# A two-layer diffusion step on one core: constants on other queues, finer first pieces of the modulation, its loads a batch ahead of their products

## The chip, the cores and the metric

One Trainium2 chip, one of its cores. The time is device microseconds (us) of one execution of the whole program, and the figure for a kernel is the median of its runs.

## The reference

Two layers over 256 tokens of 2048 columns: 128 context tokens (group 0) and 128 latent tokens (group 1). All weights are fp32 and each is used once in a step. Cut to what matters here:

```
mod    = silu(c) @ w_mod + b_mod                 # w_mod: 2048 x 12288 a layer; six segments of 2048
shift1, scale1, gate1, shift2, scale2, gate2 = split(mod, 6)
h      = rmsnorm(x, norm1) * (1 + scale1) + shift1
proj   = h @ w_in                                # 2048 x 4640
mix    = concat(attention(proj), gated_linear_attention(proj)) @ w_out      # 2048 x 2048
x      = x + gate1 * mix
h2     = rmsnorm(x, norm2) * (1 + scale2) + shift2
x      = x + gate2 * (relu(h2 @ w_up) ** 2 @ w_down)      # 2048 x 8192 and back
```

The two groups have conditioning vectors of their own (`c_ctx` and `c`). Nothing of a layer's projection can start before shift1 and scale1 of the columns that it contracts over are there.

## The kernel before

**Weights.** A weight matrix is read in chunks of 256 rows and 512 columns (512 KB) into `raw`, one of eight buffers of the pool `rawp`. `split` (L106 to 108) makes two fp32r parts of a chunk: ScalarE rounds it (`wh`, L107), VectorE subtracts (`wl`, L108). `block` (L304) computes 512 output columns: for each chunk and each group, six products into a PSUM tile `acc`, namely `wh` with the high and the low part of x (`TH`, `TL`; L345, L346) and `wl` with `TH` (L347), for two rows of 128. A full block of eight chunks has 96 such products.

**Modulation.** `w_mod` goes through the same eight buffers as `rawm`, on the same SyncE queue. A load of 512 KB feeds two products of 32 columns of TensorE (L219, L237). The generator `on_pe` yields after each load and its products; `pump` advances it by so many loads. `block` calls it beside its chunks, in batches of at least `BATCH` = 4, by a share per block that the table `N_MOD` sets for each stage; `need` advances it until what is asked for is there. `mod_first` (L227) makes shift1 and scale1 of layer 0 in four quarters of four 128-row chunks; `mod_pe` (L209) makes a segment of 2048 columns in 32 loads. Layer 0's segments 2, 4 and 3 and layer 1's 4 and 3 are made in this way; the others are summed by VectorE beside the MLP (`mod_dve`, L254).

**Stages of layer 0.** The head: constants, silu of the conditioning vectors, x normalised and transposed into `xT0` (L397 to 411), the first quarter of the modulation. Stage a: nine blocks of `w_in` over chunk rows 0 to 3, then nine over rows 4 to 7, kept as partial sums `part` (L427, L429). Stage b: the nine blocks over rows 8 to 15, with attention and linear attention as side work of the blocks. Then the output projection (four blocks of `w_out`, the second norm behind the last of them), and the MLP. In layer 1 the projection is one stage, c, of nine full blocks.

**What sets the order.** SyncE issues every weight load, in program order as the scheduler of the build left it. Each engine executes its own list in order. A load waits for the buffer that it takes over, and the loads of the SyncE and ScalarE queues share eight completion semaphores in turn, so that the ninth load waits until the first has landed. GpSimd's queue carries masks, x, head norms and caches (`load`, L68). The lists of the engines are shown below where the change moves them.

Of the kernel before, what the change touches and what calls it, by code (L numbers as in the profile page):

```python
# [50 lines left out]
def trunk(tc, nc, I, O):  # L51
    with ExitStack() as st:
# [18 lines left out]
        # tiles of 4 KB a partition; a tag's slots are shared by tiles that live one after the other  # L71
# [19 lines left out]
        nc.sync.dma_start(ident, I["ident"])  # L91
# [5 lines left out]
        # column 1 of ones: from column 1 - g on it sums over the partitions into row g  # L97
# [12 lines left out]
        def rstd(ss, n, count):  # L110
            """(ss / count + EPS) ** -0.5: by exp and log, then a Newton step"""
# [20 lines left out]
        crow = etile((32, P), "crow")  # L132
        nc.sync.dma_start(crow[0:16], I["c_ctx"].rearrange("(k p) -> k p", p=P))
        nc.sync.dma_start(crow[16:32], I["c"].rearrange("o (k p) -> (o k) p", p=P))
# [9 lines left out]
        # columns (k, g); a product takes 32 of them from (k, 0) on and uses its first two rows  # L144
# [4 lines left out]
        # per layer: columns of b_mod, norm1, norm2 and of the gate biases  # L149
        cols, gcols, modc, gdram = [], [], [], []  # L150
        for l in range(L):
            rows = etile((P, P), "rows")
            nc.sync.dma_start(rows[0:96], I["b_mod"][l].rearrange("(k p) -> k p", p=P))
            nc.sync.dma_start(rows[96:112], I["norm1"][l].rearrange("(k p) -> k p", p=P))
            nc.sync.dma_start(rows[112:128], I["norm2"][l].rearrange("(k p) -> k p", p=P))
            grow = etile((8, P), "grow")
            nc.sync.dma_start(grow[0:4], I["b_gate_fwd"][l].rearrange("(k p) -> k p", p=P))
            nc.sync.dma_start(grow[4:8], I["b_gate_bwd"][l].rearrange("(k p) -> k p", p=P))
# [9 lines left out]
        # modulation: a segment of 2048 columns, as columns of modc; either all on the tensor engine, or  # L168
        # with the sums over the row chunks on the vector engine
# [20 lines left out]
        def mod_turn(ps):  # L190
            """four transposes in place"""
            pt = ps.rearrange("p (j t) -> p j t", t=P)
            for h in range(2):
# [4 lines left out]
            return pt  # L198
# [11 lines left out]
        def mod_pe(l, seg):  # L210
            ps = ps_mod.tile([P, 512], F32, tag="mod", name="mod")
            for kc in range(KC):
                for half in range(2):
# [3 lines left out]
                    for cc in range(2):  # L217
                        q = half * 2 + cc
                        nc.tensor.matmul(ps[32 * q:32 * q + 32, :], CT[:, 2 * kc:2 * kc + 32], raw[:, cc * 512:(cc + 1) * 512],  # L219
                                         start=kc == 0, stop=kc == KC - 1)  # L220
                    if kc < KC - 1 or half < 1:
                        yield
            mod_columns(l, seg, ps)
            yield

        def mod_first(l, q):
            """a quarter of the columns of shift1 and scale1, in sums over the even and over the odd row chunks"""  # L227
            ps = ps_mod.tile([P, 512], F32, tag="mod", name="mod")
            for ch in range(KC // 2):
                for a in range(2):  # L230
                    raw = rawp.tile([P, 2, 512], F32, tag="raw", name="rawm")
                    c0 = a * D + q * 512
                    nc.sync.dma_start(raw, I["w_mod"][l, ch * 256:(ch + 1) * 256, c0:c0 + 512]
                                      .rearrange("(c p) n -> p c n", p=P))
                    for k in range(2):
                        r = 32 * (a * 2 + k)
                        nc.tensor.matmul(ps[r:r + 32, :], CT[:, 4 * ch + 2 * k:4 * ch + 2 * k + 32], raw[:, k],  # L237
                                         start=ch == 0, stop=ch == KC // 2 - 1)
                    if ch < KC // 2 - 1 or a < 1:
                        yield  # L240
            pt = mod_turn(ps)
            pv = pt.rearrange("p j (c r) -> p c r j", r=32)
            ks = slice(q * 4, q * 4 + 4)
            for a in range(2):
                m = modc[l][:, a, :, ks]
# [46 lines left out]
        def pump(gen, n=1):  # L292
            for _ in range(n):
                next(gen, None)
# [602 lines left out]
```

## Time and profile before

| | |
|---|---|
| runs | 2413.26, 2414.18, 2421.23 us; median 2414.18 |
| profiled execution, first to last instruction | 2416.7 us (the trace gives no time for it beside this span) |
| TensorE busy | 2352.2 us, 97% of the span |
| granted TensorE clock, mean | 0.990 |
| moved by DMA | 613.20 MB, mean 254 GB/s |

How to read it: a busy TensorE row is not TensorE at its peak, since the records of matmuls overlap; the distance from the start of one to the start of the next says what one costs. The profiled execution lies 2.5 us above the median of the runs.

### The profile page before, as it was taken

To read this page: it belongs to the slowest core of one execution; us is meant where nothing else is said; L and a number is where in the kernel's file an instruction comes from. 1 tells how busy PE (TensorE), PEld (TensorE's weight loads), DVE (VectorE), ACT (ScalarE), POOL (GpSimd) and SP (SyncE) were. 2 spreads that over 40 slices of the span, in tenths; PEclk is the share of its full clock that TensorE was granted. 3 is DMA by queue.
4 is the path that set the end of the run, shared out by engine and by line. 5 is a ranking of instruction groups with operands and counts; after the bars stand their busy time and mean duration, and the time that the engine had idled before them with its cause. 6 is when DMAs were issued, how large, how long until landed. Compare 5 with 4: busy or idle time off the path is not lost.

```text
span 2416.7 us, 32872 instructions
## 1 busy us (share of the span) xinstructions
PE 2352.2 (97%) x12533; PEld 1778.1 (74%) x12533; DVE 1635.4 (68%) x1936; ACT 1090.3 (45%) x1470; POOL 192.0 (8%) x253
## 2 busy tenths in 40 slices
PE   6999999989999999999999999999999999999998
PEld 2655555767878878878876767777788888888887
DVE  3444774558998999959976675556898445454455
ACT  2423443545544534534544555455554443443542
POOL 1000341100000000000010432010000000000001
PEclk9999999998999999999999999999999999999999
DMA  8899878885889989858887577788688656656654
GB/s 299 270 335 332 288 277 281 284 290 191 297 301 310 303 278 309 296 184 296 302 273 256 184 233 230 245 263 263 227 287 279 190 177 202 189 183 191 193 179 182
DMA packets 274334, 613.20 MB, mean 254 GB/s; under 512 B 24273, under 2 KB 24785, under 8 KB 274177
## 3 DMA queue, kind: packets, MB, share of 16 engines
q1 hardware_dynamic: 264048, 579.63, 72.2%
q0 software_dynamic: 10128, 31.48, 4.4%
q8 instruction: 98, 1.61, 0.3%
q14 instruction: 60, 0.48, 0.1%
HBM read 601.01 MB, written 10.03 MB: 253 GB/s over the span
## 4 chain that ended last, share of the span: by engine, by line
PE 86%; DVE 4%; DMA 4%; issue 3%; POOL 1%; ACT 1%; SPq 0%; POOLq 0%; DVEq 0%; ACTq 0%
PE acc L345 25%; PE acc L347 25%; PE acc L346 25%; PE mod L219 4%; PE mod L237 2%; DVE wl L108 1%; DMA rawm<-in_w_mod_dram 1%; DMA raw<-in_w_up_dram 1%; PE aT L104 1%; DMA raw<-in_w_down_dram 1%; DVE ga L270 1%; DMA rows<-in_b_mod_dram 1%; PE sc L577 1%; PE mod L277 1%; PE xnT L104 1%
## 5 line engine op out<-in xcount | busy, mean ns | idle before, releaser
L108 DVE TENSOR_TENSOR wl<-raw,wh 128x1024 fp32r<-128x1024 f32 (+1 forms) x586 | 692.1, 1189 | 423.6 <-ACT wh L107 407.4
L107 ACT CAST wh<-raw 128x1024 fp32r<-128x1024 f32 (+1 forms) x586 | 592.4, 1017 | 785.1 <-PE acc L346 623.8
L345 PE MATMUL acc<-wh,TH 128*128 128x512 f32 x2248 | 892.8, 398 | 1.1 <-ACT wh L107 1.0
L346 PE MATMUL acc<-wh,TL 128*128 128x512 f32 x2248 | 882.5, 393 | 0.4 <-DVE TL L108 0.4
L347 PE MATMUL acc<-wl,TH 128*128 128x512 f32 x2248 | 862.4, 396 | 1.6 <-DVE wl L108 1.6
L345 PEld LDWEIGHTS acc<-wh,TH 128*128 128x128 f32 x2248 | 423.7, 189 | 139.5 <-issue 27.3
L347 PEld LDWEIGHTS acc<-wl,TH 128*128 128x128 f32 x2248 | 422.8, 189 | 126.4 <-issue 16.6
L346 PEld LDWEIGHTS acc<-wh,TL 128*128 128x128 f32 x2248 | 423.9, 189 | 94.0 <-issue 6.8
L270 DVE SCALAR_TENSOR_TENSOR ga<-rawm,CT,ga 128x1024 f32<-128x1024 f32 x300 | 378.1, 1278 | 28.8 <-DMA rawm<-in_w_mod_dram 27.7
L108 DVE TENSOR_TENSOR wx<-raw,wx 128x1024 fp32r<-128x1024 f32 (+1 forms) x182 | 194.5, 1079 | 102.8 <-ACT wx L107 102.7
L107 ACT CAST wx<-raw 128x1024 fp32r<-128x1024 f32 (+1 forms) x182 | 168.0, 937 | 192.6 <-PE acc L346 146.2
L345 PE MATMUL acc<-wx,TH 128*128 128x512 f32 x632 | 247.6, 392 | 0.0
L346 PE MATMUL acc<-wx,TL 128*128 128x512 f32 x632 | 246.9, 391 | 0.0
L347 PE MATMUL acc<-wx,TH 128*128 128x512 f32 x632 | 239.6, 390 | 0.0
L345 PEld LDWEIGHTS acc<-wx,TH 128*128 128x128 f32 x632 | 119.5, 189 | 25.9 <-issue 0.8
L346 PEld LDWEIGHTS acc<-wx,TL 128*128 128x128 f32 x632 | 119.4, 189 | 25.1
L347 PEld LDWEIGHTS acc<-wx,TH 128*128 128x128 f32 x632 | 119.2, 189 | 25.1
L219 PE MATMUL mod<-rawm,CT 128*32 128x512 f32 x640 | 115.8, 610 | 4.4 <-DMA rawm<-in_w_mod_dram 2.5
L237 PE MATMUL mod<-rawm,CT 128*32 128x512 f32 x256 | 58.2, 653 | 18.9 <-DMA rawm<-in_w_mod_dram 18.9
L185 POOL DMA_DIRECT2D gd<-gs x4 | 2.1, 522 | 884.6 <-DVE gs L184 884.6
L219 PEld LDWEIGHTS mod<-rawm,CT 128*32 128x32 f32 x640 | 18.9, 109 | 45.0 <-issue 40.0
L812 ACT ACTIVATE relu<-acc 128x512 f32<-128x512 f32 x64 | 37.9, 592 | 30.4 <-PE acc L347 30.4
(242 smaller groups left out, 1343.2 us busy)
## 6 DMA issues: line engine op xcount, KB each, us to landing
rawm<-in_w_mod_dram SPq DMA_DIRECT2D x384, 512.0 KB, 5.5
raw<-in_w_up_dram SPq DMA_DIRECT2D x256, 512.0 KB, 4.6
raw<-in_w_down_dram SPq DMA_DIRECT2D x256, 512.0 KB, 5.3
raw<-in_w_in_dram SPq DMA_DIRECT2D x144, 512.0 KB, 5.3
raw<-in_w_out_dram SPq DMA_DIRECT2D x64, 512.0 KB, 7.8
gx<-gd POOLq DMA_DIRECT2D x32, 256.0 KB, 7.3
x1d<-x POOLq DMA_DIRECT2D x16, 256.0 KB, 5.0
gx<-x1d POOLq DMA_DIRECT2D x16, 256.0 KB, 8.6
```

What stands on the lines that cost most here:

```text
L104: nc.tensor.transpose(dst[:, j], s, ident)
L107: nc.scalar.copy(hi, v)
L108: nc.vector.tensor_tensor(out=lo, in0=v, in1=hi.bitcast(F32), op=ALU.subtract)
L219: nc.tensor.matmul(ps[32 * q:32 * q + 32, :], CT[:, 2 * kc:2 * kc + 32], raw[:, cc * 512:(cc + 1) * 512], start=kc == 0, stop=kc == KC - 1)
L237: nc.tensor.matmul(ps[r:r + 32, :], CT[:, 4 * ch + 2 * k:4 * ch + 2 * k + 32], raw[:, k], start=ch == 0, stop=ch == KC // 2 - 1)
L270: nc.vector.scalar_tensor_tensor(out=ga[g], in0=raw, scalar=c, in1=ga[g], op0=ALU.mult, op1=ALU.add)
L277: nc.tensor.matmul(ps[32 * q:32 * q + 32, :], unit[:, 1 - g:33 - g], acc[q // 2][g][:, (q % 2) * 512:(q % 2) * 512 + 512], start=g == 0, s ...
L345: nc.tensor.matmul(acc[g], xh, wh[:, k, :], start=first, stop=False)
L346: nc.tensor.matmul(acc[g], xl, wh[:, k, :], start=False, stop=False)
L347: nc.tensor.matmul(acc[g], xh, wl[:, k, :], start=False, stop=final)
L577: nc.tensor.matmul(sps[hh][w_ * c:w_ * c + w_, n], EB[r, n % 4, j0:j0 + w_], EA[r, n % 4, i0:i0 + w_], start=True, stop=True, tile_positio ...
L812: nc.scalar.activation(r, acc, AF.Relu)
```

## The change

Three things. The identity and the conditioning vectors are loaded from ScalarE's queue and the rows of biases and norms from GpSimd's (into one tile, `rowt`); x is loaded from SyncE's queue, ahead of the first `w_mod` load. `mod_first` makes pieces of 2, 2, 4, 4 and 4 row chunks (a load of a piece of two is 512 rows of 256 columns, still 512 KB), and stage a has three rounds of nine blocks, over 1, 1 and 2 chunks. The generators yield the products as a function: `pump` first runs those of the loads issued before (`flush`), then issues new loads. The shares in `N_MOD` are new.

```diff
-N_MOD = dict(a=(2, 4), b=9.25, out0=4, c=6, out1=3)
+N_MOD = dict(a=(1, 2, 3.6), b=7, out0=8.25, c=6, out1=3)
+FIRST = ((0, 2), (2, 4), (4, 8))
 BATCH = 4
...
-        nc.sync.dma_start(ident, I["ident"])
+        nc.scalar.dma_start(ident, I["ident"])
...
-        nc.sync.dma_start(crow[0:16], I["c_ctx"].rearrange("(k p) -> k p", p=P))
-        nc.sync.dma_start(crow[16:32], I["c"].rearrange("o (k p) -> (o k) p", p=P))
+        rowt = big("PM", (P, 8, P), "rowt")
+        crow = rowt[0:32, 0]
+        nc.scalar.dma_start(crow[0:16], I["c_ctx"].rearrange("(k p) -> k p", p=P))
+        nc.scalar.dma_start(crow[16:32], I["c"].rearrange("o (k p) -> (o k) p", p=P))
+        x0 = []
+        for g, n in enumerate(("x_prompt", "x_sample")):
+            x0.append([big("E", name="x0") for _ in range(2)])
+            for h in range(2):
+                nc.sync.dma_start(x0[g][h], I[n][0][:, h * 1024:(h + 1) * 1024])
...
-            nc.sync.dma_start(rows[0:96], I["b_mod"][l].rearrange("(k p) -> k p", p=P))
+            load(rows[0:96], I["b_mod"][l].rearrange("(k p) -> k p", p=P))
...
-        on_pe = mods([(mod_first, 0, q) for q in range(4)]
+        on_pe = mods([(mod_first, 0, k0, k1 - k0) for k0, k1 in FIRST + ((8, 12), (12, 16))]
...
+        loaded = []
+
+        def flush():
+            while loaded:
+                loaded.pop(0)()
 
         def pump(gen, n=1):
+            if gen is on_pe:
+                flush()
             for _ in range(n):
-                next(gen, None)
+                products = next(gen, None)
+                if products is not None:
+                    loaded.append(products)
 
         def need(*what):
             gen = on_dve[0] if what in ON_DVE[0] else on_dve[1] if what in ON_DVE[1] else on_pe
+            if gen is on_pe and what not in have:
+                flush()
             while what not in have:
-                pump(gen)
+                pump(gen, BATCH if gen is on_pe else 1)
+                if gen is on_pe:
+                    flush()
...
-        for q in range(4):
-            need(0, "first", q)
...
+        for i, (k0, k1) in enumerate(FIRST):
+            first(k0, k1)
             for c0 in PIECES:
...
-                block(TH, TL, I["w_in"][0][:, c0:c0 + 512], None, keep, N_MOD["a"][q], [2 * q, 2 * q + 1])
+                block(TH, TL, I["w_in"][0][:, c0:c0 + 512], None, keep, N_MOD["a"][i], list(range(k0 // 2, k1 // 2)))
+        for k0 in (8, 12):
+            first(k0, k0 + 4)
```

SyncE's list at the start. Before, from the second layer's rows of constants on (the same five for layer 0 stand ahead of them, three `w_mod` loads ahead of those, and the identity and the conditioning vectors first of all):

```order
L153 DMA rows<-in_b_mod_dram 96x128
L154 DMA rows<-in_norm_dram 16x128
L155 DMA rows<-in_norm_dram 16x128
L157 DMA grow<-in_b_gate_fwd_dram 4x128
L158 DMA grow<-in_b_gate_bwd_dram 4x128
L233 DMA rawm<-in_w_mod_dram 128x2x512 x13
L320 DMA raw<-in_w_in_dram 128x2x512 x4
L233 DMA rawm<-in_w_mod_dram 128x2x512 x4
```

The same queue in the changed kernel, from its first load on:

```order
L142 DMA x_106<-in_x_prompt_dram 128x1024
L142 DMA x_107<-in_x_prompt_dram 128x1024
L142 DMA x_110<-in_x_sample_dram 128x1024
L142 DMA x_111<-in_x_sample_dram 128x1024
L244 DMA rawm<-in_w_mod_dram 128x4x256 x8
L351 DMA raw<-in_w_in_dram 128x2x512 x4
L244 DMA rawm<-in_w_mod_dram 128x4x256 x4
L351 DMA raw<-in_w_in_dram 128x2x512 x4
```

No constant stands on this queue any more, and the first chunk of `w_in` is its thirteenth load.

ScalarE's list at the start, in which `junk` are the sums of squares of x (x_151, x_152 are the prompt's halves, x_208, x_209 the sample's), `y` the two steps of the root, `wh` the rounding of a chunk of `w_in`, `xv` and `TH` the modulated x. Before:

```order
L387 ACTIVATE junk,ss<-x_151 128x512 x2
L387 ACTIVATE junk,ss<-x_152 128x512 x2
L115 ACTIVATE y<-v 128x1
L116 ACTIVATE y<-y 128x1
L387 ACTIVATE junk,ss<-x_208 128x512 x2
L387 ACTIVATE junk,ss<-x_209 128x512 x2
L115 ACTIVATE y<-v 128x1
L116 ACTIVATE y<-y 128x1
L107 CAST wh<-raw 128x1024 x3
L379 ACTIVATE xv<-xT_150,modc_130 128x128 x4
```

The changed kernel (x_110, x_111 are the sample's halves):

```order
L117 ACTIVATE y<-v 128x1
L118 ACTIVATE y<-y 128x1
L109 CAST wh<-raw 128x1024
L418 ACTIVATE junk,ss<-x_110 128x512
L109 CAST wh<-raw 128x1024
L418 ACTIVATE junk,ss<-x_110 128x512
L418 ACTIVATE junk,ss<-x_111 128x512 x2
L109 CAST wh<-raw 128x1024
L117 ACTIVATE y<-v 128x1
L118 ACTIVATE y<-y 128x1
L410 ACTIVATE xv<-xT_154,modc_136 128x128 x2
```

The roundings of the first three chunks of `w_in` now stand between and behind the sample's sums of squares, ahead of its root.

TensorE's list at the end of the third block of `w_out` in layer 0 and the start of the fourth (two rows of `mod<-rawm` are one load's products). Before:

```order
L345 MATMUL acc_4044<-wx,TH 128x512
L346 MATMUL acc_4044<-wx,TL 128x512
L347 MATMUL acc_4044<-wx,TH 128x512
L345 MATMUL acc_4232<-wh,TH 128x512
L346 MATMUL acc_4232<-wh,TL 128x512
L347 MATMUL acc_4232<-wl,TH 128x512
```

The changed kernel:

```order
L376 MATMUL acc_4064<-wx,TH 128x512
L377 MATMUL acc_4064<-wx,TL 128x512
L378 MATMUL acc_4064<-wx,TH 128x512
L230 MATMUL mod<-rawm,CT 32x512 x18
L205 MATMUL mod<-ident,modt 128x128 x4
L230 MATMUL mod<-rawm,CT 32x512 x6
L376 MATMUL acc_4312<-wh,TH 128x512
L377 MATMUL acc_4312<-wh,TL 128x512
```

Twelve loads' products and the four transposes that end a segment now stand between the two blocks; on SyncE the twelve loads stand between the last four chunks of `w_out` of the third block and the first four of the fourth.

## Rows read from the trace of the kernel before

**Rows 1.** The page: busy us, share of the span and instructions of each engine.

```profile
PE 2352.2 (97%) x12533; PEld 1778.1 (74%) x12533; DVE 1635.4 (68%) x1936; ACT 1090.3 (45%) x1470; POOL 192.0 (8%) x253
```

**Rows 2.** Windows by stage: the head, the two rounds of stage a, stage b, the output projection with the second norm. Columns: stretch, its length, busy time of PE, PEld, DVE, ACT, POOL (with counts), granted clock, DMA share, GB/s.

```profile
0.00:50.40 50.40, 26.28 (x109) 7.36 (x109) 19.65 (x53) 13.47 (x31) 8.03 (x18) 0.94 0.90 307
50.40:120.00 69.60, 69.60 (x306) 42.97 (x304) 24.61 (x31) 30.01 (x41) 0.00 (x0) 0.97 0.81 268
120.00:198.00 78.00, 76.95 (x349) 43.08 (x346) 39.39 (x61) 23.49 (x31) 0.58 (x1) 1.00 0.96 339
198.00:422.00 224.00, 217.59 (x1924) 123.76 (x1923) 135.92 (x219) 88.56 (x148) 56.54 (x62) 0.98 0.83 290
422.00:540.00 118.00, 111.58 (x534) 81.02 (x533) 69.26 (x107) 57.70 (x96) 15.96 (x29) 1.00 0.87 288
```

**Rows 3.** The timeline of TensorE in stage a at three places: start, length, line, operation.

```profile
59.91 0.39 PE L346 MATMUL acc<-wh,TL 128*128 128x512 f32 x1
60.14 0.39 PE L347 MATMUL acc<-wl,TH 128*128 128x512 f32 x1
60.45 1.07 PE L237 MATMUL mod<-rawm,CT 128*32 128x512 f32 x8
61.45 0.50 PE L345 MATMUL acc<-wh,TH 128*128 128x512 f32 x1
61.79 0.39 PE L346 MATMUL acc<-wh,TL 128*128 128x512 f32 x1
...
66.80 0.39 PE L347 MATMUL acc<-wl,TH 128*128 128x512 f32 x1
67.12 1.05 PE L237 MATMUL mod<-rawm,CT 128*32 128x512 f32 x4
68.10 0.50 PE L345 MATMUL acc<-wh,TH 128*128 128x512 f32 x1
...
157.03 0.39 PE L346 MATMUL acc<-wh,TL 128*128 128x512 f32 x1
157.35 1.92 PE L237 MATMUL mod<-rawm,CT 128*32 128x512 f32 x16
159.20 0.50 PE L347 MATMUL acc<-wl,TH 128*128 128x512 f32 x1
```

**Rows 4.** The timeline of SyncE's queue at the start: start, time until the last of the group was issued.

```profile
2.12 1.46 SPq L233 DMA_DIRECT2D rawm<-in_w_mod_dram  x3
3.62 1.24 SPq L153 DMA_DIRECT2D rows<-in_b_mod_dram  x1
18.96 0.31 SPq L155 DMA_DIRECT2D rows<-in_norm_dram  x1
19.83 0.29 SPq L158 DMA_DIRECT2D grow<-in_b_gate_bwd_dram  x1
20.16 11.51 SPq L233 DMA_DIRECT2D rawm<-in_w_mod_dram  x13
```

**Rows 5.** What SyncE's queue waited for in the first 50 us: total, times, longest.

```profile
SPq L155 <- DMA rawm<-in_w_mod_dram: 7.0, 1, 7.0
```

**Rows 6.** Windows of 4 us in the head (columns as in rows 2).

```profile
0.00:4.00 4.00, 0.00 (x0) 0.00 (x0) 0.33 (x4) 1.28 (x1) 2.93 (x9) 1.00 0.35 73
12.00:16.00 4.00, 1.58 (x4) 0.00 (x0) 0.00 (x0) 0.00 (x0) 0.90 (x2) 1.00 1.04 177
32.00:36.00 4.00, 3.85 (x24) 2.00 (x24) 3.43 (x11) 0.00 (x0) 0.00 (x0) 1.00 1.05 387
```

**Rows 7.** The timeline of the head from the sample's sums of squares to the first product of a block (all engines, lines left out).

```profile
29.86 0.61 ACT L387 ACTIVATE junk<-x 128x512 f32<-128x512 f32 x1
31.26 0.14 DVE L113 TENSOR_SCALAR v<-s 128x1 f32<-128x1 f32 x1
32.50 1.67 DVE L408 TENSOR_SCALAR xn<-x,r 128x512 f32<-128x512 f32 x4
34.09 1.28 DVE L411 COPY xT<-xnT 128x512 f32<-128x512 f32 x2
...
43.07 1.04 ACT L107 CAST wh<-raw 128x1024 fp32r<-128x1024 f32 x1 [11.19 <-DMA raw<-in_w_in_dram]
44.15 1.22 DVE L108 TENSOR_TENSOR wl<-raw,wh 128x1024 fp32r<-128x1024 f32 x1
48.87 1.14 ACT L107 CAST TH<-xv 128x512 fp32r<-128x512 f32 x2
50.46 1.65 PE L345 MATMUL acc<-wh,TH 128*128 128x512 f32 x3
```

**Rows 8.** What TensorE waited for over the whole program.

```profile
PE xnT L104 <- DVE xn L368: 10.1, 5, 6.5
PE kaT L638 <- DVE part L613: 3.7, 1, 3.7
PE qaT L104 <- DVE part L625: 2.7, 2, 2.2
```

**Rows 9.** The timeline of SyncE's queue in the output projection of layer 0.

```profile
492.30 12.23 SPq L216 DMA_DIRECT2D rawm<-in_w_mod_dram  x4
505.61 11.36 SPq L320 DMA_DIRECT2D raw<-in_w_out_dram  x6
```

**Rows 10.** DMA issues: KB of each, median us from issue to landing.

```profile
raw<-in_w_up_dram SPq DMA_DIRECT2D x256, 512.0 KB, 4.6
```

More of the change, by code (lines that the diff above doesn't have):

```diff
@@ L216, in mod_pe @@
                     nc.sync.dma_start(raw, I["w_mod"][l, kc * P:(kc + 1) * P, c0:c0 + 1024])
[L217 to L223, printed above, removed]
@@ L224, in mod_pe, with products @@
-            yield
-        def mod_first(l, q):
+                    def products(kc=kc, half=half, raw=raw):
+                        for cc in range(2):
+                            q = half * 2 + cc
+                            nc.tensor.matmul(ps[32 * q:32 * q + 32, :], CT[:, 2 * kc:2 * kc + 32],
+                                             raw[:, cc * 512:(cc + 1) * 512], start=kc == 0, stop=kc == KC - 1)
+                        if kc == KC - 1 and half == 1:
+                            mod_columns(l, seg, ps)
@@ L228, in mod_first @@
+                    yield products
+        def mod_first(l, k0, nk):
             ps = ps_mod.tile([P, 512], F32, tag="mod", name="mod")
[L229 removed]
+            n, per = nk * P, 8 // nk
+            for ch in range(KC // per):
                 for a in range(2):
[L231 to L233 removed]
+                    raw = rawp.tile([P, per, n], F32, tag="raw", name="rawm")
+                    c0 = a * D + k0 * P
+                    nc.sync.dma_start(raw, I["w_mod"][l, ch * per * P:(ch + 1) * per * P, c0:c0 + n]
@@ L251, in mod_first, with products @@
-            nc.vector.scalar_tensor_tensor(out=m, in0=m, scalar=1.0, in1=nrm.unsqueeze(1).to_broadcast([P, 2, 4]),
-                                           op0=ALU.add, op1=ALU.mult)
-            have.add((l, "first", q))
-            yield
+                    def products(ch=ch, a=a, raw=raw):
+                        for k in range(per):
+                            kc = ch * per + k
+                            r = 32 * (a * 2 + k % 2)
+                            nc.tensor.matmul(ps[r:r + 32, 0:n], CT[:, 2 * kc:2 * kc + 32], raw[:, k],
+                                             start=kc < 2, stop=kc >= KC - 2)
+                        if ch == KC // per - 1 and a == 1:
+                            finish()
@@ new lines, in finish @@
+                    def finish():
+                        pt = mod_turn(ps, nk)
+                        pv = pt.rearrange("p j (c r) -> p c r j", r=32)
+                        for a in range(2):
+                            m = modc[l][:, a, :, k0:k0 + nk]
+                            bias = cols[l][:, a * 16 + k0:a * 16 + k0 + nk]
+                            nc.vector.tensor_tensor(out=m, in0=pv[:, 2 * a, 0:2],
+                                                    in1=bias.unsqueeze(1).to_broadcast([P, 2, nk]), op=ALU.add)
+                            nc.vector.tensor_tensor(out=m, in0=pv[:, 2 * a + 1, 0:2], in1=m, op=ALU.add)
+                        nrm = cols[l][:, 96 + k0:96 + k0 + nk]
+                        m = modc[l][:, 1, :, k0:k0 + nk]
+                        nc.vector.scalar_tensor_tensor(out=m, in0=m, scalar=1.0,
+                                                       in1=nrm.unsqueeze(1).to_broadcast([P, 2, nk]),
+                                                       op0=ALU.add, op1=ALU.mult)
+                        have.add((l, "first", k0))
@@ L256, in mod_dve @@
+                    yield products
         def mod_dve(l, seg):
```

64 lines of the change are left out of this document (22 added, 42 removed).

## The prediction

> **What bounds the kernel now.** First the page's engine row [rows 1]: TensorE is busy for 97% of the span, so a change counts where it shortens TensorE's list or fills a hole in it. Then the windows by stage [rows 2]. In the first 50.40 us TensorE is busy for 26.28; in both rounds of stage a, and but for 6.4 us in stage b, it has no idle time. DMA is close behind: 339 GB/s at a share of 0.96 in the second round, 288 at 0.87 in the output projection. So there are three questions: when the first product of a block starts, how much stands in TensorE's list after it, and whether the loads keep up.
>
> What stands in the list is read from the timeline [rows 3]. Products of a block start 0.23 us apart (59.91 to 60.14). The products of one `w_mod` load between them make that 1.30 us (66.80 to 68.10), those of two loads 1.31 (60.14 to 61.45), those of four 2.17 (157.03 to 159.20); the product behind comes after 0.34 instead of 0.23 (61.45 to 61.79). So an interruption costs 0.33 us by itself and 0.86 for each pair of loads: 1.19 for one or two, 2.05 for three or four. One load alone costs as much as two together. Check: stage a has 432 products of blocks, 98 us, and by its list 33 interruptions with 38 pairs, 33 x 0.33 + 38 x 0.86 = 43.6; together 142 of the 147.6 us that the windows give. Stage a is TensorE's.
>
> The head is read from SyncE's queue [rows 4]: three `w_mod` loads by 3.58 us, then nothing but constants until 20.16. Issuing one constant takes 0.3 us, one took 1.24; the rest is waiting, 7.0 us of it for a `w_mod` load to land [rows 5], since a load waits for the semaphore of the eighth load before it. In those 4 us (12 to 16) DMA moved 177 GB/s, against 387 later [rows 6].
>
> **The head.** The first product starts at 50.46 [rows 7], behind 16 loads of a quarter. Now it needs x (4 loads), 8 loads of a piece, the first chunks of `w_in`, and by TensorE's list four loads of the second piece. At 387 GB/s a load of 0.524 MB takes 1.35 us [rows 6]. The first chunk of `w_in` is the 13th load, 17.6 us; the constants and small tables beside it, some 0.7 MB by their shapes, 1.9; the first 4 us move only 73 GB/s, a loss of 3.2; a slow stretch like that at 12 us loses 2.2. It lands at 24.9. The loads alone would let a block start at 24.9 + 7 x 1.35 + 1.1 = 35.5. ScalarE's list sets it later: rounding (1.04), a square (0.61), rounding, three squares, rounding end at 30.5; VectorE subtracts (1.22) and goes on at 31.8 with the sample's root. From there 1.24 us to the scaled x (31.26 to 32.50), 1.67 for four of them, 1.28 for two copies, and some 1.1 for modulating and rounding (estimated from 1.14 for rounding twice as much) [rows 7]: 37.1. Gain 50.5 - 37.1 = **13.4 us**; ends 10.5 (the slow stretch twice) and 17 (no slow stretch, chain by the loads).
>
> **Stage a.** By the new list 24 interruptions with 35 pairs: 24 x 0.33 + 35 x 0.86 = 38.0, **5.6 us** less. At the start of the third round the modulated columns come late: six loads' products (2.9 us) cover a chain of VectorE and ScalarE of 3 to 6 us (rounding to first product alone took 1.6 [rows 7]); I take **+1.5**, ends 0 and 3. Eighteen more additions of partial sums, each half the size of the subtraction of 1.22 us [rows 7], lie on VectorE, which is busy for 64 of the 147.6 us [rows 2]: nothing; without that cover they would be 11 us.
>
> **Stage b.** The share falls from 9.25 to 7 loads a block. 33 interruptions with 62 pairs (64.2 us) become 18 with 43 (42.9): **21.3 us** less. Products of `w_mod` also fill holes in which TensorE would wait for the side work; the waits that showed were 3.7 and 2.7 us [rows 8]. I take **+2** of new waits, ends 0 and 11.
>
> **Output projection of layer 0.** What left stage b arrives here. 6 interruptions with 11 pairs (11.5 us) become 9 with 27; without the twelve loads at the fourth block that is 20.2, **+8.7**. At the fourth block the segments 3 and 4 aren't complete: 64 + 96 = 160 loads are needed, and the shares have given 8 + 9 + 18 + 32.4 + 63 + 24.75 = 155. So `need` issues two batches, and with the batch before them twelve loads stand on SyncE ahead of the fourth block's first chunk. The first of them takes a buffer whose product stands 12 products of a block and two pairs ahead of the third block's end, 4.6 us; it lands after between 1.35 us (its own transfer) and 4.6 us (the median of a load [rows 10]), I take 3; twelve more follow at 1.35: the chunk is there 14.6 us after the third block's end, rounded at some 15.5. Before, the two blocks followed each other without a hole, SyncE having issued four loads and then `w_out` [rows 9]. So **+15.5**, ends 7 (the products alone: 0.33 + 7 x 0.86 and the transposes) and 21 (at 331 GB/s, see below).
>
> The Trainium skill, "DMA: Bandwidth & Descriptors", section Specifications, gives some 358 GB/s as the limit of HBM for a core. By that a load takes 1.46 us, the head gains 1.5 us less, the hole is 1.3 us longer, and the sum would be -3.1. The trace shows 387 GB/s over 4 us [rows 6], so I keep 1.35.
>
> **The rest.** In the MLP one interruption goes (**-1.2**); four loads' products now stand inside the second norm, where TensorE waited anyway (10.1 us over both layers [rows 8]), and cost nothing unless that wait is gone (1.7). Stage c of layer 1 handles about as many loads in worse groups: 11 interruptions with 35 pairs become 21 with 39, **+6.7**; its output projection **+1.2**.
>
> **Sum.** -13.4 - 5.6 + 1.5 - 21.3 + 2 + 8.7 + 15.5 - 1.2 + 6.7 + 1.2 = **-5.9 us**. Against the profiled 2416.7 us that is 2410.8; against the median of the runs, 2414.18, which is 2.5 lower, **2408**. A measurement of this kernel can tell about 0.3%, 7.2 us: 2406.9 to 2421.4 counts as no change. By its sum the change moves 48 us about and keeps 6.
>
> **The rivals.**
>
> A. The hole at the fourth block stays near its products' own 7 us, because the loads before it come earlier than I place them. For it: the queue waits for buffers most of the time, so little has to be won. Against it: thirteen loads of 1.35 us in a row can't be hidden behind 4.6 us of products. It gives 8.5 us more: 2400.
>
> B. Stage b doesn't shorten by what is taken out of its list, because the side work (scores by levels, attention) sets its end. For it: the two waits for VectorE [rows 8] and TensorE's idle 6.4 us of 224 [rows 2]. Against it: VectorE, ScalarE and GpSimd are busy there for 136, 89 and 57 of 224 us. With 11 us of new waits instead of 2: 2417.
>
> C. DMA becomes the bound. Place: stage a and the output projection. Stage a would have 95 loads, 49.8 MB, in 143.5 us, 347 GB/s; the output projection 75 loads and 6.3 MB of gates, x and stores, 45.6 MB, in about 142. Point from which it decides: some 345 GB/s. For it: 288 GB/s at a share of 0.87 makes 331 at a full share [rows 2]. Against it: 387 in the head, where SyncE's loads are almost alone [rows 6]. At 331, stage a takes 150 us (+7) and the output projection 138 and the norm's wait behind it (+6): 2408 + 13.5 = 2422, slower than before.
>
> **How the numbers follow.** The forecast has 0.40, A 0.23, B 0.15, C 0.22. The forecast's own terms (head 10.5 to 17, hole 7 to 21) spread it from 2400 to 2417; of its 0.40 some 0.17 lie below 2406.9 and little above 2421.4. With A that makes 0.41 for faster; B and the rest of the forecast, with a third of C, 0.39 for no change; the rest of C and the tails 0.20 for slower. The range runs from A's lower part to C's upper, 2396 to 2424.
>
> **What would show it.** Right: the first product of a block near 37 us; stage b starting near 181 us instead of 198 and taking some 204 us instead of 224; a hole of 12 to 18 us in TensorE's products of blocks between the third and fourth block of `w_out`, with SyncE issuing twelve `w_mod` loads; stage c longer by some 7 us. Wrong: a first product before 33 or after 41; SyncE or DMA named as what TensorE waited for in stage a; stage b shorter by less than 12; no hole at the fourth block; or a stage of the MLP that differs, which the change doesn't touch.

## The result, and the profile after

| | before | changed |
|---|---|---|
| median of the runs, us | 2415.81 (4 runs, the three above and 2417.44) | 2440.55 (4 runs, 2435.14 to 2451.98) |
| profiled span, us | 2416.7 | 2440.8 |
| granted clock, mean | 0.990 | 0.982 |

The ratio is 1.011, 95% interval 1.0081 to 1.0138: slower by 25 us, where 2408 was forecast with a range up to 2424. The forecast was wrong.

The page's engine row, beside [rows 1]: TensorE has 5.5 us more of work in a span that is 24.1 longer.

```profile
PE 2357.7 (97%) x12597; PEld 1790.2 (73%) x12597; DVE 1648.0 (68%) x1961; ACT 1087.8 (45%) x1472; POOL 196.5 (8%) x259
```

The windows by stage, beside [rows 2] (same columns): head, stage a in two parts, stage b to the middle of the first block of `w_out`, a hole, the rest of the output projection with the norm.

```profile
0.00:42.80 42.80, 24.22 (x135) 11.18 (x136) 17.72 (x49) 11.85 (x29) 11.29 (x24) 0.84 1.00 319
42.80:120.00 77.20, 76.04 (x370) 48.05 (x369) 41.53 (x61) 32.16 (x46) 0.00 (x0) 1.00 0.87 294
120.00:190.00 70.00, 66.56 (x308) 41.12 (x307) 34.78 (x52) 19.51 (x22) 0.57 (x1) 0.98 0.93 331
190.00:397.00 207.00, 200.77 (x1865) 127.43 (x1864) 136.75 (x210) 91.13 (x151) 61.33 (x62) 0.98 0.78 271
397.00:436.00 39.00, 26.97 (x164) 13.96 (x162) 19.08 (x48) 17.48 (x34) 7.44 (x13) 0.83 0.78 274
436.00:560.00 124.00, 110.14 (x483) 73.29 (x484) 60.23 (x92) 44.83 (x76) 9.09 (x17) 0.91 0.86 298
```

The fifth row is new: 39 us in which TensorE is busy for 27 and its granted clock is 0.83, with DMA at a share of 0.78. The same stretch in TensorE's timeline (lines left out; `op` are gla_out's products, L765 and L768, `ogT` the transposes of its result):

```profile
397.08 0.39 PE L378 MATMUL acc<-wx,TH 128*128 128x512 f32 x1
397.31 1.95 PE L765 MATMUL op<-part,ST 128*128 128x128 f32 x16
399.19 2.78 PE L230 MATMUL mod<-rawm,CT 128*32 128x512 f32 x24
411.06 3.64 PE L230 MATMUL mod<-rawm,CT 128*32 128x512 f32 x8 [9.10 <-DMA rawm<-in_w_mod_dram]
414.63 0.80 PE L765 MATMUL op<-part,ST 128*128 128x128 f32 x2
415.36 0.79 PE L768 MATMUL op<-s,qs 64*128 64x128 f32 x4
...
428.48 1.05 PE L230 MATMUL mod<-rawm,CT 128*32 128x512 f32 x4
432.08 1.45 PE L230 MATMUL mod<-rawm,CT 128*32 128x512 f32 x4 [2.55 <-DMA rawm<-in_w_mod_dram]
433.64 1.97 PE L106 MATMUL ogT<-ident,part 128*128 128x128 f32 x8
435.88 0.79 PE L376 MATMUL acc<-wh,TH 128*128 128x512 f32 x1 [0.28 <-ACT TH L109]
```

The second half of this block contracts over gla_out's result, so no product of a block can stand between 397.08 and 435.88. Before, gla_out stood among the products of O_G's blocks. Its second part now waits 9.10 us behind a load, and SyncE's queue shows why that load is late (start, time until the last of the group was issued):

```profile
385.52 18.50 SPq L351 DMA_DIRECT2D raw<-in_w_out_dram  x4
404.11 2.75 SPq L225 DMA_DIRECT2D rawm<-in_w_mod_dram  x4
406.91 5.59 SPq L351 DMA_DIRECT2D raw<-in_w_out_dram  x4
413.03 12.85 SPq L225 DMA_DIRECT2D rawm<-in_w_mod_dram  x4
```

The four loads were issued from 404.11 on, behind four chunks of `w_out` that took 18.5 us to issue.

The load is not the only thing that came late there. The second part needs the buffers of the first, which VectorE frees when it has scaled them (`gla`), and for that it needs the two steps of the root on ScalarE. Those stand in ScalarE's list among the roundings of `w_out`, which waited for the same queue's chunks:

```profile
407.00 0.20 ACT L117 ACTIVATE y<-v 128x4 f32<-128x4 f32 x1
409.80 1.04 ACT L109 CAST wx<-raw 128x1024 fp32r<-128x1024 f32 x1 [2.60 <-DMA raw<-in_w_out_dram]
410.75 0.20 ACT L118 ACTIVATE y<-y 128x4 f32<-128x4 f32 x1
413.08 1.11 DVE L773 SCALAR_TENSOR_TENSOR gla<-op,r,hn 128x128 f32<-128x128 f32 x4
```

So the products at 414.63 could not have started before some 414.2 even without the late load: two paths, both behind late chunks of SyncE's queue, end within half a microsecond. No run parts them.

What TensorE waited for in the whole program, beside [rows 8]:

```profile
PE mod L230 <- DMA rawm<-in_w_mod_dram: 15.4, 5, 9.1
PE xnT L106 <- DVE xn L399: 11.6, 5, 6.4
PE mod L251 <- DMA rawm<-in_w_mod_dram: 10.2, 4, 4.3
PE cps L144 <- DMA rowt<-in_c_dram: 7.0, 1, 7.0
```

The foreseen hole ahead of the fourth block, in TensorE's timeline: 501.13 to 516.56, 15.43 us.

```profile
501.13 0.39 PE L378 MATMUL acc<-wx,TH 128*128 128x512 f32 x1
501.45 3.85 PE L230 MATMUL mod<-rawm,CT 128*32 128x512 f32 x28
...
509.30 1.05 PE L230 MATMUL mod<-rawm,CT 128*32 128x512 f32 x4 [2.71 <-DMA rawm<-in_w_mod_dram]
...
516.56 0.80 PE L376 MATMUL acc<-wh,TH 128*128 128x512 f32 x1
```

The block's first chunk of `w_out` was rounded as it landed, 14.1 us after the third block's last product:

```profile
515.20 1.14 ACT L109 CAST wh<-raw 128x512 fp32r<-128x512 f32 x2 [11.41 <-DMA raw<-in_w_out_dram]
```

Where the time went is read best from marks that every kernel has. Each is the start of an instruction in the trace; behind a slash the difference to before. The stores are those of the first group's `x1d`, the relus those of the first group.

| mark, us | before | changed | old shares (e1) | shares alone (e6) | b = 8 (e5) | no w_mod in b (e9) |
|---|---|---|---|---|---|---|
| first product of a block | 50.5 | 42.8 / -7.7 | 43.0 / -7.5 | 50.1 / -0.3 | 41.5 / -9.0 | 41.7 / -8.7 |
| last partial sum of stage a | 198.2 | 189.7 / -8.5 | 189.5 / -8.7 | 197.3 / -0.9 | 186.9 / -11.3 | 187.3 / -10.8 |
| store of `w_out`'s block 1 | 464.8 | 451.8 / -13.0 | 449.9 / -14.9 | 469.0 / +4.3 | 443.0 / -21.8 | 415.0 / -49.8 |
| store of block 3 | 515.1 | 501.9 / -13.2 | 493.3 / -21.8 | 519.7 / +4.7 | 494.2 / -20.8 | 463.3 / -51.8 |
| first relu of layer 0 | 572.9 | 582.5 / +9.6 | 551.4 / -21.5 | 584.2 / +11.3 | 562.2 / -10.7 | 512.1 / -60.9 |
| last relu of layer 0 | 1198.7 | 1209.2 / +10.6 | 1173.9 / -24.7 | 1209.2 / +10.5 | 1188.2 / -10.4 | 1137.6 / -61.1 |
| first relu of layer 1 | 1709.7 | 1734.0 / +24.3 | 1696.4 / -13.3 | 1727.3 / +17.6 | 1710.4 / +0.7 | 1673.1 / -36.6 |
| end | 2416.7 | 2440.8 / +24.1 | 2402.8 / -13.9 | 2434.1 / +17.4 | 2416.7 / 0.0 | 2379.4 / -37.2 |

### The profile page after: what moved, and what is told of

Same layout as the page of the kernel before. It is cut to its first block, busy times and chain, and to the rows that moved or that the text cites. A ratio compares the mean times of both kernels' runs of the same rounds, so it can differ in the third digit from the quotient of the medians.

```text
span 2440.8 us, 32987 instructions
## 1 busy us (share of the span) xinstructions
PE 2357.7 (97%) x12597; PEld 1790.2 (73%) x12597; DVE 1648.0 (68%) x1961; ACT 1087.8 (45%) x1472; POOL 196.5 (8%) x259
## 4 chain that ended last, share of the span: by engine, by line
PE 85%; DMA 6%; DVE 4%; issue 3%; ACT 1%; POOL 1%; SPq 0%; POOLq 0%; DVEq 0%; ACTq 0%
PE acc L376 25%; PE acc L378 25%; PE acc L377 24%; PE mod L230 4%; DMA rawm<-in_w_mod_dram 3%; PE mod L251 2%; DVE wl L110 1%; DVE ga L287 1%; DMA raw<-in_w_up_dram 1%; PE aT L106 1%; DMA raw<-in_w_down_dram 1%; PE sc L609 1%; DMA raw<-in_w_in_dram 1%; PE mod L294 1%; PE S L690 0%
## 5 line engine op out<-in xcount | busy, mean ns | idle before, releaser
L378 PEld LDWEIGHTS acc<-wl,TH 128*128 128x128 f32 x2248 | 423.5, 189 | 119.2 <-DVE wl L110 11.0
L230 PE MATMUL mod<-rawm,CT 128*32 128x512 f32 x640 | 121.9, 621 | 15.8 <-DMA rawm<-in_w_mod_dram 15.4
L251 PE MATMUL mod<-rawm,CT 128*32 128x512 f32 (+1 forms) x320 | 53.4, 565 | 11.4 <-DMA rawm<-in_w_mod_dram 10.2
L844 ACT ACTIVATE relu<-acc 128x512 f32<-128x512 f32 x64 | 37.9, 592 | 28.3 <-PE acc L378 28.2
```

The source lines that it names most:

```text
L251: nc.tensor.matmul(ps[r:r + 32, 0:n], CT[:, 2 * kc:2 * kc + 32], raw[:, k], start=kc < 2, stop=kc >= KC - 2)
L378: nc.tensor.matmul(acc[g], xh, wl[:, k, :], start=False, stop=final)
L844: nc.scalar.activation(r, acc, AF.Relu)
```

## The experiments

Theory S was that the new shares cost, by the two holes. Its rival Q was that the loads issued a batch ahead hold their buffers longer and starve the weights. Times are medians; a ratio is to the kernel before on the same chip, with its 95% interval. The experiments ran on several chips; the median of the kernel before lay between 2415.81 and 2417.99 us on them, so differences of a few us between two chips are not told apart. Lengths by marks are of one profiled execution each.

### Which part of the change costs

**e1**, the changed kernel with the old shares:

```diff
-N_MOD = dict(a=(1, 2, 3.6), b=7, out0=8.25, c=6, out1=3)
+N_MOD = dict(a=(1, 2, 3.6), b=9.25, out0=4, c=6, out1=3)
```

> The changed kernel with the shares of before in stage b (9.25) and in the output projection (4). Theory S (the new shares): they put 14 loads' products and all of gla_out's products in one hole of 38.8 us behind the first half of w_out's first block, and 12 loads' products in another of 15.4 us ahead of the fourth block. With the old shares TensorE's list has gla_out's products in three places between products of blocks and no large group ahead of the fourth block; stage b gets some 10 us longer. Expected 2418 (2412 to 2425). Theory Q (the loads a batch ahead hold their buffers longer and starve the weights): the groups in stage b keep waiting, 2435 to 2445.

2407.37, ratio 0.9964 (0.9952 to 0.9976): below S's 2412 to 2425. S counted stage b some 10 us longer with 14 loads more; from the end of stage a to the first store it was 1.7 us shorter (260.4 against 262.1).

**e2**, products right behind their loads again:

```diff
-                if products is not None:
-                    loaded.append(products)
+                if products is not None:
+                    products()
...
```

(The flushes go as well, and `need` advances load by load again.)

> The changed kernel with each load's products right behind it, as before; everything else as changed. Theory S: gla_out stays in one hole (12 loads' products instead of 14), ahead of the fourth block stand 5 loads' products instead of 12; the second hole falls from 15.4 to some 8, the first stays over 25: 2432 (2426 to 2440). Theory Q: no load holds a buffer across a batch, TensorE's waits for w_mod loads (15.4 and 10.2 us over the program) mostly go: 2415 to 2422.

2434.38, ratio 1.0075 (1.0057 to 1.0094).

**e3**, the identity, the conditioning vectors, the rows (`load` replaced) and x back on their old queues:

```diff
-        nc.scalar.dma_start(ident, I["ident"])
+        nc.sync.dma_start(ident, I["ident"])
...
-            load(rows[0:96], I["b_mod"][l].rearrange("(k p) -> k p", p=P))
+            nc.sync.dma_start(rows[0:96], I["b_mod"][l].rearrange("(k p) -> k p", p=P))
```

> The changed kernel with the constants on SyncE's queue and x on GpSimd's again. Both theories: only the head differs (TensorE's list is the same from stage b on), so the 7.7 us that the first product of a block gained are given back, or more, since the finer piece's products come behind the constants: first product at 46 to 52, time 2444 to 2450. If the head's gain is lost again later (loads that are the bound afterwards), the time stays at 2440.

2450.22, ratio 1.0158 (1.012 to 1.0196). The first product came at 43.8, earlier than the 46 to 52 expected, and stage a ended at 194.9, 5.2 us later than in the changed kernel.

**e4**, quarters:

```diff
-FIRST = ((0, 2), (2, 4), (4, 8))
+FIRST = ((0, 4), (4, 8))
-N_MOD = dict(a=(1, 2, 3.6), ...
+N_MOD = dict(a=(2, 4), ...
```

> The changed kernel with the first pieces of four row chunks each and two rounds in stage a (shares 2 and 4 a block). The first product comes later than 42.8 (16 loads instead of 8 ahead of it, 8 x 1.35 us = some 10 us more: 50 to 54), but stage a has one round less of partial sums and no wait at the third round. Ahead of the fourth block 7 loads' products stand instead of 12, in the lump with gla_out 8 instead of 14. Theory S: 2436 (2430 to 2444). If the finer pieces cost by themselves (a third round of stage a that waits for its modulation), 2428 or less.

2430.29, ratio 1.0067 (1.0041 to 1.0092). The first product came at 46.9, not at 50 to 54, so the pieces are worth less in the head than I wrote. Stage a ended where it did before (198.2).

**e6**, before with the new shares alone, and **e7**, before with the constants moved alone (the edits of e1 and e3 in the other direction):

> The kernel before with the new shares of stage b (7) and of the output projection (8.25), and nothing else of the change. Theory S (the shares cost by themselves): gla_out's products fall into one hole behind the first half of w_out's first block, with 5 loads' products; no large group ahead of the fourth block; slower than before by 10 to 20, 2428 to 2438. Theory X (the shares cost only together with the batch ahead and the finer pieces, which use up the buffers): 2410 to 2420.

2436.78, ratio 1.0078 (1.0063 to 1.0093).

> The kernel before with the constants off SyncE's queue and x on it ahead of w_mod, and nothing else. 16 loads of a quarter still stand ahead of the first product: 46 to 48 us instead of 50.5. If the gain of the head is kept through stage a: 2413 to 2415; if stage a, which shares its loads' rate with the head, gives it back (as where the quarters came back in the changed kernel: first product 3.5 us earlier, stage a ending where it did before), 2417 to 2419.

2413.85, ratio 0.9992 (0.9977 to 1.0007), no difference. The first product came at 47.8, the end of stage a at 197.0.

**e8**, the changed kernel with e1's and e2's edits together:

> The kernel before with the constants moved and the finer first pieces: old shares, products right behind their loads. If the batch ahead adds nothing to what the old shares gave (2407): 2404 to 2411, with stage a ending near 190. If it is the batch ahead that shortens the output projection there (it ended 13 us earlier against before than stage b did): 2414 to 2422.

2404.97, ratio 0.9945 (0.993 to 0.9959).

So the new shares cost, as S had it, and Q falls. They cost 33 us in the changed kernel (2440.55 against 2407.37), 29 without the batch ahead (2434.38 against 2404.97), 19 alone. That the two holes make this cost is shown for the second alone: of the 38 us between e1 and the changed kernel in the profiled executions 29 lie between the first store of `w_out` and the first relu, and only 1.7 between the end of stage a and the first store, where the first hole is and 14 loads fewer pay for it. The batch ahead gains nothing: beside the old shares 2407 with it and 2405 without, beside the new ones 6 us slower with it, and both pairs' intervals overlap. Constants and finer pieces gain more together than apart: the end of stage a moves by -3.3 (pieces without constants, e3), by -1.2 (constants without pieces, e7; in e4 by 0.0) and by -8.5 with both.

### What the shares cost, and where

**e5**, `b=8` in place of `b=7`:

> The changed kernel with a share of 8 instead of 7 in stage b: nine loads more are done by the fourth block of w_out, so that none is forced ahead of it; gla_out's products still stand behind O_G's blocks in one hole with 8 loads' products (14 in the changed kernel). Theory S1 (the forced loads at the fourth block are the larger part of the loss): 2441 less the 15.4 us hole, plus one more interruption each for the moved loads: 2424 (2420 to 2430). Theory S2 (the hole with gla_out behind O_G's blocks is the larger part): 2432 to 2440.

2420.66, ratio 1.0019 (1.0007 to 1.0032): as S1 had it, 20 us under the changed kernel. Of its profiled execution's gain 11.5 us lie between the first store and the first relu, 6.0 between the end of stage a and the first store. The hole at the fourth block is gone, and the first hole is 23.2 us long instead of 38.8.

**e9**, no `w_mod` in stage b and the output projection:

```diff
+        def mod_none(l, seg):
+            def products():
+                nc.vector.memset(modc[l][:, seg], 0.5)
+                mod_finish(l, seg)
+            yield products
...
-                     + [(mod_pe, l, s) for l in range(L) ...
+                     + [(mod_none if l == 0 else mod_pe, l, s) for l in range(L) ...
-N_MOD = dict(a=(1, 2, 3.6), b=7, out0=8.25, c=6, out1=3)
+N_MOD = dict(a=(1, 2, 3.6), b=0, out0=0, c=6, out1=3)
```

> The changed kernel without the loads and products of layer 0's segments 2, 4 and 3 (constants stand in for them): no w_mod load in stage b nor in the output projection of layer 0. From the end of stage a to the store of w_out's first block the changed kernel took 262 us with 61 loads in stage b, the kernel before 267 with 82. Theory L (TensorE's list sets the length, 0.33 us for an interruption and 0.86 for a pair of loads): 262 less 18 x 0.33, 31 x 0.86 and the 11.7 us of waits for w_mod loads: some 218 us. Theory K (the chain of the side work, with gla_out at its end, sets the length): 240 to 258 us, gla_out again in a hole behind the first half of w_out's first block, TensorE waiting in it for VectorE and ScalarE.

One run, 2381.22; constants stand in for the segments, so it does not compute the step. From the end of stage a to the first store it took 415.0 - 187.3 = 227.7 us: between L's 218 and K's 240, nearer to L, so neither the list nor the side work alone sets the length. The nine blocks of stage b end early, at 322.5, and what stands behind them up to the first store takes 92.5 us. There the side work leaves holes. The windows of stage b, the last two around gla_out:

```profile
187.00:240.00 53.00, 50.70 (x243) 40.58 (x242) 34.63 (x59) 27.35 (x38) 5.11 (x7) 1.00 0.59 179
297.00:330.00 33.00, 29.29 (x489) 22.42 (x488) 30.74 (x36) 17.18 (x29) 17.12 (x11) 0.97 0.45 144
330.00:370.00 40.00, 27.77 (x347) 20.09 (x347) 18.77 (x38) 14.76 (x35) 11.66 (x21) 0.72 0.22 67
370.00:399.00 29.00, 21.72 (x100) 16.80 (x98) 15.37 (x44) 13.42 (x30) 7.29 (x13) 0.60 0.35 110
```

Between 330 and 399 TensorE idles for 19.5 of 69 us and its clock is 0.60 to 0.72. Over all the windows it idles for 28.9 of 228 us, and its waits name VectorE and ScalarE for 28.2 of them. In stage b the products of `w_mod` stand partly in such holes. The price of a load follows from the marks and from the loads whose products TensorE's list has between them. Up to the first store the old shares (e1) take 260.4 us with 92 loads, (260.4 - 227.7) / 92 = 0.36 us each; the new ones take 262.1 with 78, 0.44 each: 14 loads fewer and 1.7 us more. From the first store to the first relu e9 takes 97.1 us with 2 loads, e6 115.2 with 24, e5 119.2 with 19, the changed kernel 130.7 with 29: 0.8, 1.3 and 1.2 for each load. These prices hold everything that comes with a load, its products, its bytes and the waits for it; e9 takes them all away at once, and no run parts them.

**e13**, the same sums given to other blocks (the table is indexed by block):

```diff
-b=7, out0=8.25
+b=(9, 9, 9, 9, 9, 9, 9, 0, 0), out0=(0, 11, 11, 11)
```

> The changed kernel with its loads of w_mod given to other blocks of the same two stages: 9 for each of the first seven blocks of stage b, none for the two of O_G and the first of w_out, 11 for each of the other three (63 and 33 in sum as before). SyncE issues 19 chunks of weights in a row there, and the seven loads whose products stand in gla_out's hole were issued before them. Theory W (it is the wait for a late load inside gla_out and the half clock behind it that cost): from the end of stage a to the first store of w_out 242 to 252 us instead of 262, no wait for w_mod in that hole; the eleven forced loads at the fourth block still cost their 14 us: 2425 to 2433. Theory P (gla_out behind O_G's blocks costs by its place): 258 to 264 us there, 2437 to 2445.

2435.24, ratio 1.0086 (1.0064 to 1.0107). The length was 446.4 - 189.1 = 257.3 us, between W's range and P's. The hole was 26.1 us, and one load in it was late after all:

```profile
PE mod L230 <- DMA rawm<-in_w_mod_dram: 4.1, 1, 4.1
PE ogT L106 <- DVE part L788: 2.5, 1, 2.5
PE op L765 <- DVE gla L773: 0.2, 1, 0.2
PE acc L376 <- ACT TH L109: 0.2, 1, 0.2
```

The waits of the other kernels' holes sum in the same way to 11.9 us (changed), 4.5 (e5) and 13.0 (e6). Length less waits: 262.1 - 11.9 = 250.2, 257.3 - 7.0 = 250.3, 256.1 - 4.5 = 251.6, and 271.7 - 13.0 = 258.7 for e6. So in three kernels the waits in the hole account for the difference. The larger ones of e6, two of them for VectorE and ScalarE:

```profile
PE mod L224 <- DMA rawm<-in_w_mod_dram: 4.5, 1, 4.5
PE ogT L106 <- DVE part L779: 4.3, 1, 4.3
PE acc L364 <- ACT TH L109: 3.5, 1, 3.5
```

e6 has in addition the half clock (the lower of TensorE's two levels, 1.2 and 2.4 GHz) through most of its hole, here from its timeline and its windows:

```profile
417.02 1.92 PE L224 MATMUL mod<-rawm,CT 128*32 128x512 f32 x4 [4.50 <-DMA rawm<-in_w_mod_dram]
418.87 0.80 PE L756 MATMUL op<-part,ST 128*128 128x128 f32 x2
419.60 1.22 PE L759 MATMUL op<-s,qs 64*128 64x128 f32 x4
420.75 0.80 PE L756 MATMUL op<-part,ST 128*128 128x128 f32 x2
```

```profile
408.00:430.00 22.00, 17.50 (x66) 10.35 (x66) 9.28 (x29) 5.17 (x12) 0.00 (x0) 0.70 0.61 203
430.00:453.00 23.00, 14.59 (x69) 8.85 (x67) 7.82 (x20) 10.64 (x22) 7.40 (x13) 0.65 0.60 164
```

After a wait of 4.50 us a pair of groups of `op` takes 1.88 us (418.87 to 420.75) instead of 1.05 in e13, where no long wait stood ahead of them (406.55 to 407.60). Eight such pairs make 8 x 0.83 = 6.6 us, most of the 8 between 258.7 and 250. This is an estimate, since the other holes have stretches at the half clock as well.

```profile
406.55 0.49 PE L765 MATMUL op<-part,ST 128*128 128x128 f32 x2
406.96 0.71 PE L768 MATMUL op<-s,qs 64*128 64x128 f32 x4
407.60 0.49 PE L765 MATMUL op<-part,ST 128*128 128x128 f32 x2
```

**e10**, `b=9`, and **e11**, e8 with `out0=6`:

> The changed kernel with a share of 9 instead of 7 in stage b, everything else as changed. In TensorE's list gla_out's products stand among the products of O_G's blocks again and no loads are forced ahead of the fourth block. If the place of gla_out and the forced loads are what the shares cost, this runs like the one with the old shares, 2403 to 2410, although the output projection still takes 8.25 loads a block. If a large share in the output projection costs by itself: 2414 to 2420.

2421.99, ratio 1.0022 (1.0011 to 1.0034): the expectation failed. The stretch up to the first store went well (448.7), but first store to first relu took 121.3 us with 23 loads: the output projection pays for a load wherever gla_out stands.

> The finer first pieces and the moved constants, products right behind their loads, shares 9.25 in stage b as before and 6 in the output projection (4 before). Stage b has the list of the run that took 2405. The output projection has 14 interruptions instead of 10 (8 loads more, +4.8 by the prices of the prediction), stage c and layer 1's output projection 11 instead of 17 with 8 loads fewer (-5.4): 2402 to 2407, no difference that three rounds can tell.

2409.26, ratio 0.997 (0.9956 to 0.9984), 4 us above e8 and above the 2402 to 2407 expected. First store to first relu took 114.6 us with 16 loads, in e8 103.5 with 9.

### Stage c

In four kernels, batches of eight loads in stage c:

```diff
-                    if due[0] >= BATCH:
+                    if due[0] >= (8 if mods_per == N_MOD["c"] else BATCH):
```

> As the run with a share of 9 in stage b, and in stage c batches of at least eight loads instead of four: 5 interruptions instead of 10 with as many loads. By the price of the prediction 5 x 0.33 = 1.7 us less than that run. If it is the interruptions that make stage c longer than before (by 7 to 14 us in all kernels but that with the constants alone): 5 us less or more.

2411.49, ratio 0.9978 (0.9966 to 0.9991), 10.5 us under e10.

> The changed kernel with batches of at least eight loads in stage c instead of four: 13 interruptions of blocks instead of 21, 48 loads instead of 50. By the prices of the prediction 8 x 0.33 + 0.9 = 3.5 us less, 2437; by what the same edit gave beside a share of 9 (10.5 us for 5 interruptions, 2.1 each): 17 us less, 2424.

2447.98, ratio 1.0133 (1.0102 to 1.0163), 7.4 us above the changed kernel.

> The change with the old shares (2407) and batches of at least eight in stage c: 15 interruptions instead of 20 in stage c and the output projection behind it. By 0.33 each 2405; by 2.1 each 2397.

2411.7, ratio 0.9984 (0.9972 to 0.9996), 4.3 us above e1.

> The finer first pieces and the moved constants with the old shares and without the batch ahead (2405), and batches of at least eight in stage c: 12 interruptions instead of 17 there. By 0.33 each 2403; by 2.1 each 2394. One of this and the run before should be the fastest of all.

2403.23, ratio 0.9943 (0.9925 to 0.9961); with e8 the fastest.

The same edit gave -10.5, +7.4, +4.3 and -1.7 us. Only the first of these is clear of noise, since e10 and e12 ran on one chip and their intervals lie apart; the other three pairs' intervals overlap. In the profiled executions the stretch from the last relu of layer 0 to the first of layer 1 moved the same ways, by -8.0, +6.6, +8.3 and -1.9. So the number of interruptions does not by itself set the length of stage c. What does stays open.

## Why the prediction was wrong

| step, us | predicted | measured by the marks |
|---|---|---|
| head | -13.4 | -7.7 |
| stage a | -4.1 | -0.8 |
| stage b to the first store of `w_out` | -19.3 | -4.5 |
| rest of the output projection and the norm | +24.2 | +22.6 |
| MLP of layer 0 | -1.2 | +1.0 |
| layer 1 up to its MLP | +7.9 | +13.7 |
| MLP of layer 1 | 0 | -0.2 |
| sum | -5.9 | +24.1 |

(The prediction booked all of the output projection behind stage b, so the fourth row takes its 8.7 and 15.5 together.)

**The step that failed is "Stage b": "33 interruptions with 62 pairs (64.2 us) become 18 with 43 (42.9): 21.3 us less", with 2 us of new waits.** By the marks it makes up 15 of the 30 us between forecast and result, and some 10 if the nine loads that went no further than the first block of `w_out` (17 loads there instead of 8) are taken out at the prediction's own price (an estimate, 9/16 of its 8.7 us). In e6, where nothing but the shares is changed, it is +5.2 instead of -19.3, and from e1 to the changed kernel +1.7.

The blocks did get shorter, more than the forecast's 204 instead of 224: from the last sum of stage a to VectorE's last sum of stage b it took 191.2 us instead of 223.6. But what stood among them came behind them. From there to the first store it took 70.9 us instead of 43.0 (in e6 86.5, in e9 92.5): gla_out's work, 14 of the loads and waits of 11.9 us stand in the hole. The prices 0.33 and 0.86 were read in stage a, where TensorE hardly waits, and used where the side work leaves holes that the loads' products fill. The prediction named both sides of it ("Products of `w_mod` also fill holes in which TensorE would wait") and priced the second at 2 us from the waits that showed before; but those are the waits that are left when 82 loads fill the holes. e9 shows the empty holes.

**Rival B** was nearest to what happened: the side work, more than the list of the blocks, set when the first store came, and its 11 us are the size of the new waits. Its cause, VectorE's chain, is borne out in part. In the changed kernel TensorE's waits name loads that SyncE had behind `w_out`; in e6 8.5 of the 13.0 us in the hole, and in e9 nearly all, name VectorE and ScalarE. **Rival C** is out for the loss: in the hole DMA's share is 0.78, from 397 to 410, where TensorE waited longest, 0.58, and e1 moves the same bytes in 33 us less. In stage a it has a small part: the wait of 2.4 us for ScalarE's rounding follows one of 5.47 us of ScalarE for a chunk of `w_in`.

**The fourth block** came as worked out: 15.43 us against 15.5, by the same twelve loads (487.97 to 504.77 on SyncE's queue) and on the path foreseen: the first chunk was rounded 14.1 us after the third block's end, where 14.6 was forecast for its landing. TensorE's own last products before the block, at the half clock (3.63 us from 513.00), end at the same time. e5, which has no forced loads, has no such hole. **Rival A** is out with it.

**The head** gained 7.7 instead of 13.4; the first product at 42.8 lies past the 41 that the prediction named as a sign of being wrong. The windows that answer to [rows 6], while the moved constants were still on other queues:

```profile
12.00:16.00 4.00, 4.00 (x25) 1.67 (x21) 2.46 (x4) 0.00 (x0) 3.21 (x6) 1.00 1.21 292
16.00:20.00 4.00, 0.41 (x4) 0.00 (x0) 0.00 (x0) 0.00 (x0) 0.00 (x0) 0.95 0.86 232
20.00:24.00 4.00, 3.53 (x16) 1.12 (x16) 0.00 (x0) 0.00 (x0) 0.00 (x0) 0.50 1.11 295
```

SyncE's queue runs without a constant, as foreseen (beside [rows 4]):

```profile
2.60 14.08 SPq L244 DMA_DIRECT2D rawm<-in_w_mod_dram  x8
16.80 6.97 SPq L351 DMA_DIRECT2D raw<-in_w_in_dram  x4
```

But 12 us at a mean of 273 GB/s instead of 387 lose 3.5 us, where 2.2 were booked; the first chunk of `w_in` was rounded at 28.76, not landed at 24.9. The forecast let rounding start with landing, and the trace has ScalarE waiting for the chunk until then, so these 3.9 us are the larger part of 5.7. ScalarE's roundings and squares then took what was counted and ended at 34.15 instead of 30.5. The other 2.0 us lie behind them, 8.65 us to the first product instead of 6.6: TensorE runs two loads of the second piece at the half clock (3.35 us at 34.45) ahead of the sample's last transposes.

**Stage a** lost 4.7 us in waits that the forecast put at 1.5: 2.4 for ScalarE's rounding, 1.2 in issue, 0.6 and 0.5 for VectorE (before 1.0 in all). That is some 2 of the 3.3 us it fell short; the rest is not accounted for. **Layer 1**: +4.6 lie between the last relu of layer 0 and the first transposes of stage c, which nothing in the forecast covered, and +9.1 from there to the MLP against 7.9. That the size was near is not evidence for its price, since the price failed in e12, e14 and e15.

The Trainium skill's 358 GB/s ("DMA: Bandwidth & Descriptors", Specifications) would, as an estimate, have put the head 1.5 us later. The traces lie on both sides of it: 386 to 395 GB/s (before) and 350 to 378 (changed) over 4 us where large loads are alone, 232 to 295 from 12 to 24 us, while the constants and small tables were on the other queues.

## What to carry to other kernels

A filler's price belongs to the stage where it is read: here 0.36 to 0.44 us for a load in stage b, where the side work leaves holes, and 0.8 to 1.3 from the first store to the first relu. Before work is taken out of a stage, ask which holes it fills; the waits that show in the profile are only those left over. And when an order is rebuilt, look in it for the first long run without a product of a block: what stands there waits on its own, and everything in it that hangs on late chunks of SyncE's queue, loads and roundings alike, can set its end.

The version to keep is e8: constants moved and finer pieces, with the old shares and without the batch ahead, 2404.97 us, 0.55% under before (e16 at 2403.23 is not told apart from it).

## What was not expected of the hardware

In e6 a wait of 4.5 us of TensorE was followed by the half clock (windows at 0.70 and 0.65 over 45 us), which hit the very chain that everything waited for: groups of 0.49 and 0.71 us took 0.80 and 1.22. The Trainium skill ("TensorE: Matmul & The Clock Gate", section HAM oscillation — how this bites in real kernels) tells of the same turn: a wait for DMA throttles the array, and the work behind it starts at the low clock; by that, the trace agrees. How long it lasts differs, and why stays open: in e6 the granted clock was 0.50 from 417 to 437 us, with TensorE's row busy throughout, and in the changed kernel, after the wait of 9.10 us, it was back at 1.00 from 416 on, some 5 us after the wait. And the large loads were slow while the constants and small tables were on other queues: in e7, whose loads have rows as long as before, DMA moved 288, 242 and 313 GB/s in the three windows from 12 to 24 us, and 388 in the next.
